# A projection step between the second and third query tile of each FoX score block, and the GLA query/key projection cut into two-bank pieces

## The chip, the cores and the metric

The kernel runs on one core of one Trainium2 chip. The metric is device microseconds (us) of one execution. The median of three runs of the kernel before is 1455.17 us (1454.29 to 1455.19).

## What is computed

One decoder layer on 512 tokens of width 1024, in float32: a half-step SwiGLU feed-forward network, a token mixer, and a second half-step feed-forward network, each between RMSNorms that are shifted, scaled and gated by a conditioning vector. The token mixer has two branches that read the same normed input `h`. Cut to what matters here:

```python
z = h @ w_in      # columns: GLA q,k,v,low-rank gate,out-gate | FoX q,k,v,forget | merge gates
logf = log_sigmoid(f_b + b_f);  F = cumsum(logf)
# FoX, 16 heads of 64, in query blocks of 128:
s = einsum('bhqd,bhkd->bhqk', q, k) * hd ** -0.5 + F[..., None] - F[:, :, None, :]
s = where(kpos <= qpos, s, -inf);  o_b = einsum('bhqk,bhkd->bhqd', softmax(s), v)
# GLA, 4 heads of 128: chunked gated linear attention o_a from q_a, k_a, v_a
merged = sigmoid(gate_a) * (o_a @ w_pa) + sigmoid(gate_b) * (o_b @ w_pb)
y = merged @ w_out
```

## The kernel before

Every large product is made of three float32r products (high by high, high by low, low by high part), each a 128x128 weight against 512 columns. Weights arrive by DMA on the SyncE queue into `raw` (four buffers), ScalarE rounds them to `whi` (L155), VectorE subtracts to `wlo` (L156), TensorE multiplies (helper `mm3`, L192; L378 in the feed-forward part).

**PSUM.** Eight banks: six rotate under the name `mm` (`acc`), two under `aux`. A new `mm` tile takes the next bank of the six, and its first matmul waits until the last reader of that bank is done.

**The filler list.** All projections of the token mixer that don't depend on the attention are cut into steps of 12 matmuls of 512 columns and put in one list, the class `Fill`. `F.run(n)` emits the next n steps and `F.until(mark)` emits steps up to a mark; the code calls these between the pieces of the attention. `F.tr` (L577) makes a projection of two tiles in 4 steps and holds two `mm` banks over them; with four tiles (as in `F.qk`, L594) it takes 8 steps and holds four banks. `F.extra` adds a step that sums one quarter of the modulation vectors: on TensorE it is 8 tiny matmuls (L268). In the list the FoX query/key projections of head pairs 1 to 7 follow each other in 4 steps each, and in front of pairs 1, 3, 5 and 7 stands one extra step.

**One head pair of FoX.** There are eight head pairs; "(k)" below means pair k. Four pieces of code work on it.

- *parts(k)* (L613, run by `evacuate`): reads the two projected banks and makes the high and low halves of q and k for both heads, on ScalarE (L617, L619, L623) and VectorE (L618, L620, L622), head 0 and then head 1.
- *scores(k)* (`fox_scores`, L728): for each of four query tiles and both heads two matmuls (L749, L750) of 128, 256, 384 and 512 columns into one `mm` bank, so eight banks in a row out of six. VectorE adds the decay bias and takes the row maximum (L753), which frees the bank.
- *soft(k)* (`fox_soft`): exponentials on ScalarE (L762), normalisation on VectorE (L766).
- *turn(k)* (`fox_turn`, L778: 18 transposes, copied by ScalarE, L780) and *out(k)* (`fox_out`, L789: the product with v; ScalarE rounds it, L198, VectorE subtracts, L199).

The main loop over p (L846 on) runs soft(p), one step, scores(p+1), steps up to a mark, turn(p), one step, out(p), parts(p+2), one more step. So two steps of the list stand between parts(p+2) and scores(p+2). The engines run their queues in order. The framework's scheduler has ordered each queue from this program order, and the order of the built program can differ from that of the code by some matmuls; every queue shown below is that of the built program.

Of the kernel before, what the change touches and what calls it, by code (L numbers as in the profile page):

```python
# [12 lines left out]
AF = mybir.ActivationFunctionType  # L13
ALU = mybir.AluOpType

P = 128
# [3 lines left out]
KD = D // P  # L20
# [3 lines left out]
QA, KA, VA, AL, RA, QB, KB, VB, FB, GA, GB = (  # L24
    0, 512, 1024, 2048, 2064, 3088, 4112, 5136, 6160, 6176, 7200)
# [14 lines left out]
def tile_hybrid_layer(  # L40
# [4 lines left out]
    nc = tc.nc  # L45
    x, out = x[0], out[0]
    w_ada, b_ada, g_pre, g_post = w_ada[0], b_ada[0], g_pre[0], g_post[0]
    w_in, w_a2, b_a, b_f, g_gla = w_in[0], w_a2[0], b_a[0], b_f[0], g_gla[0]
# [9 lines left out]
    def nm(s):  # L58
        uid[0] += 1
        return f"{s}_{uid[0]}"  # L60

    def unit(dt=F32, shape=(P, 512)):
        return sb.tile(list(shape), dt, tag="u", bufs=NU, name=nm("u"))

    def tmp(shape=(P, 512), dt=F32):
        return sb.tile(list(shape), dt, tag="t2", bufs=NTMP, name=nm("t2"))
# [4 lines left out]
    def acc(shape=(P, 512)):  # L71
        return pm.tile(list(shape), F32, tag="mm", name=nm("mm"))
# [4 lines left out]
    def small(n, tag="sm", bufs=16):  # L77
        return sb.tile([P, n], F32, tag=tag, bufs=bufs, name=nm(tag))
# [237 lines left out]
    def h_tiles():  # L316
        return [(unit(F32R), unit(F32R)) for _ in range(KD)]
# [119 lines left out]
    hs = h_tiles()  # L437
# [86 lines left out]
    hs = nxt[-1]  # L524
# [7 lines left out]
    class Fill:  # L532
# [61 lines left out]
        def qk(self, qc, kc, scale, dst):  # L594
# [7 lines left out]
                    dst.append((q, k))  # L602
            self.tr([(w_, e, lambda: hs) for e in range(2) for w_ in (qw, kw)], evac)

        def qk_parts(self, qc, kc, scale, dst):


            qw, kw = Block(w_in, 0, KD, qc, P), Block(w_in, 0, KD, kc, P)

            def evac(ps):  # L610
                late.append(lambda: parts(*ps))

            def parts(q, k):  # L613
                qx, ky, kx = [(unit(F32R), unit(F32R)) for _ in range(3)]
                for e in range(2):
                    n, o = halves[e], halves[1 - e]
                    nc.scalar.copy(ky[e][n], k[n])  # L617
                    nc.vector.tensor_tensor(kx[e][n], k[n], ky[e][n].bitcast(F32), ALU.subtract)  # L618
                    nc.scalar.activation(qx[e][n], q[n], AF.Copy, scale=scale)  # L619
                    nc.vector.scalar_tensor_tensor(qx[e][o], q[n], scale, qx[e][n].bitcast(F32),  # L620
                                                   ALU.mult, ALU.subtract)
                    nc.vector.tensor_copy(kx[e][o], ky[e][n])  # L622
                    nc.scalar.copy(ky[e][o], kx[e][n])  # L623
                dst.append((qx, ky, kx))
            self.tr([(w_, 0, lambda: hs) for w_ in (qw, kw)], evac)

    F = Fill()
# [6 lines left out]
    fqk = []  # L634
# [81 lines left out]
    def packed():  # L716

        return unit(), unit(), unit(F32, (P, 256))

    def s_at(u, i):  # L720

        return (u[1][:, 384:512], u[2], u[1][:, 0:384], u[0])[i]
# [2 lines left out]

        return (u[0], u[1][:, 0:384], u[2], u[1][:, 384:512])[j]

    def fox_scores(p, qx, ky, kx):  # L728
        S, nmx, rs = [], [], []
        for e in range(2):  # L730
            h = 2 * p + e
            fb = tmp()
            nc.sync.dma_start(fb, Fd[h].partition_broadcast(P))
            s = packed()
            for i in range(NT):
                n = (i + 1) * P
                nc.gpsimd.tensor_scalar(s_at(s, i), fb[:, 0:n], -1.0, Ft[:, i, h:h + 1], ALU.mult, ALU.add)  # L737
                dg = s_at(s, i)[:, n - P:n]
                nc.gpsimd.tensor_tensor(dg, dg, mneg, ALU.add)
            S.append(s)  # L740
            nmx.append(small(4))
            rs.append(small(4))
        for i in range(NT):
            n = (i + 1) * P
            sps = []
            for e in range(2):
                ts = slice(i * P, (i + 1) * P)
                sp = acc()
                nc.tensor.matmul(sp[:, 0:n], qx[e][:, ts], ky[e][:, 0:n], start=True, stop=False)  # L749
                nc.tensor.matmul(sp[:, 0:n], qx[e][:, ts], kx[e][:, 0:n], start=False, stop=True)  # L750
                sps.append(sp)
            for e in range(2):
                nc.vector.tensor_tensor_reduce(s_at(S[e], i), sps[e][:, 0:n], s_at(S[e], i), 1.0, -3e38,  # L753
                                               ALU.add, ALU.max, nmx[e][:, i:i + 1])
        return S, nmx, rs

    def fox_soft(state):
        S, nmx, rs = state
        for e in range(2):
            nc.vector.tensor_scalar(nmx[e], nmx[e], -1.0, None, ALU.mult)  # L760
            for i in range(NT):
                nc.scalar.activation(s_at(S[e], i), s_at(S[e], i), AF.Exp, bias=nmx[e][:, i:i + 1],  # L762
                                     accum_out=rs[e][:, i:i + 1])
            nc.vector.reciprocal(rs[e], rs[e])
            for i in range(NT):
                nc.vector.tensor_scalar(s_at(S[e], i), s_at(S[e], i), rs[e][:, i:i + 1], None, ALU.mult)  # L766

    def fox_turn(state):
        S = state[0]
        PT = []  # L770
        for e in range(2):
            pt = packed()
            for js in ((0,), (1, 3), (2,)):
                tp = (acc if e and 0 in js else aux)()
                off = 0
                for j in js:
                    for i in range(j, NT):
                        nc.tensor.transpose(tp[:, off:off + P], s_at(S[e], i)[:, j * P:(j + 1) * P], ident)  # L778
                        off += P
                nc.scalar.copy(pt[(0, 1, 2)[js[0]]][:, 0:off], tp[:, 0:off])  # L780
            PT.append(pt)
        return PT

    def fox_out(p, PT):
        po = acc()
        for j in range(NT):
            for e in range(2):
                h = 2 * p + e
                nc.tensor.matmul(po[64 * e:64 * e + 64, j * P:T], vb[j][h // 8][:, (h % 8) * 64:(h % 8 + 1) * 64],  # L789
                                 p_at(PT[e], j), start=j == 0, stop=j == NT - 1)  # L790
        o = (unit(F32R), unit(F32R))
        hilo(o[0], o[1], po)
        ob.append(o)
# [6 lines left out]
    marks = [F.mark()]  # L800
# [7 lines left out]
    def gate_b(db):  # L808
        gw = Block(w_in, 0, KD, GB + db * 256, 256)

        def evac(ps):
            for p_ in ps:
                g = unit()
                nc.scalar.activation(g, p_, AF.Tanh, scale=0.5)
                gb.append(g)
        F.tr([(gw, 0, lambda: hs), (gw, 1, lambda: hs)], evac)

    def merge_b(db):
        pw = Block(w_pb, 0, KD, db * 256, 256)

        def evac(ps):
            for p_ in ps:
                m = gb[len(mb)]
                nc.vector.scalar_tensor_tensor(m, m, 1.0, p_, ALU.add, ALU.mult)
                mb.append(m)
        F.tr([(pw, 0, lambda: ob), (pw, 1, lambda: ob)], evac)

    gqk = []
    F.qk(QA, KA, P ** -0.5, gqk)
    start_b = F.mark()  # L830
    for db in range(4):
        gate_b(db)
        merge_b(db)
    end_b = F.mark()

    def evacuate():
        while late:
            late.pop(0)()

    F.until(marks[0])  # L840
    evacuate()
    F.until(marks[1])
    st = [fox_scores(0, *fqk[0])]
    evacuate()
    F.run(1)
    for p in range(8):  # L846
        fox_soft(st[p])
        if p < 7:
            F.run(1)
            st.append(fox_scores(p + 1, *fqk[p + 1]))  # L850
        if p < 6:
            F.until(marks[p + 2] - 1)
        elif p == 7:
            F.run(4)
        PT = fox_turn(st[p])
        F.run(1)
        fox_out(p, PT)
        evacuate()
        if p == 5:
            ra2 = tmp()  # L860
            tc.keep_in_program_order(nc.sync.dma_start(ra2[0:16], w_a2))
            wa2, fill_wa2 = stacked((0, 1, 0))
            fill_wa2(ra2[0:16])
        if p < 7:
            F.run(1)

    F.until(start_b + 8)


    B, rest = [], []  # L870
# [179 lines left out]
    for h in range(4):  # L1050
# [4 lines left out]
        def fill(li):  # L1055
            F.run(2 if h == 0 or li < 4 else 1)
            if li == 0 and prev:
                prev.turn()
            if li == 4 and h < 3:
                if h == 1:  # L1060
                    F.until(gqk_end)
                nxt_hd.append(heads[h + 1]())
                nxt_hd[0].prep()
# [77 lines left out]
```

## Time and profile before

| | |
|---|---|
| median of three runs | 1455.17 us |
| the profiled execution | 1452.96 us |
| its span, first to last instruction | 1451.2 us |
| TensorE busy | 1399.9 us, 96% |
| VectorE, ScalarE, GpSimd busy | 765.7, 531.4, 203.8 us |
| mean granted TensorE clock | 0.989 of 2.4 GHz |

All stretches below are us from the start of the span. The feed-forward networks fill 0 to 420 and 1065 to the end. The FoX scores run from 500 to 650. The profile gives a start and a length for every instruction, and for idle time of an engine the event that ended it.

### The profile page before, as it was taken

How to read it: one execution, taken by the hardware profiler on the slowest of the kernel's cores; microseconds unless marked ns; L12 is line 12 of the kernel's file. 1: busy time of each engine (PE TensorE's matmuls, PEld its weight loads, DVE VectorE, ACT ScalarE, POOL GpSimd, SP SyncE). 2: the span in 40 equal slices, each digit the busy share in tenths (PEclk: the TensorE clock that was granted, in tenths of full speed). 3: DMA queues.
4: the chain of work that ended last, by engine and by line, in shares of the span. 5: the costliest groups of instructions: out<-in, count | busy, mean ns of one | idle time of the engine just before them, and what ended most of it. 6: DMA issues, size and time to landing. Idle time of an engine off the chain costs nothing.

```text
span 1451.2 us, 17081 instructions
## 1 busy us (share of the span) xinstructions
PE 1399.9 (96%) x6477; PEld 1124.3 (77%) x6477; DVE 765.7 (53%) x1210; ACT 531.4 (37%) x915; POOL 203.8 (14%) x328
## 2 busy tenths in 40 slices
PE   4899999999999999999999999999999999999998
PEld 3688888878877777767888887788888888887886
DVE  6945544372266689762745546538464334337232
ACT  5332322232244376653723333423353322222221
POOL 6200000000041643340110202100060000000001
PEclk7999999999999999999999999999999999999999
DMA  9444543272235846212232232125613223325411
GB/s 323 156 147 145 156 148 102 59 246 99 90 120 163 241 135 182 82 40 91 87 106 84 59 87 59 59 73 163 204 55 116 87 91 100 100 87 184 136 58 58
DMA packets 156463, 173.36 MB, mean 119 GB/s; under 512 B 8778, under 2 KB 123574, under 8 KB 156380
## 3 DMA queue, kind: packets, MB, share of 16 engines
q1 hardware_dynamic: 156380, 172.26, 38.4%
q8 instruction: 51, 0.84, 0.2%
q14 instruction: 32, 0.26, 0.1%
HBM read 168.00 MB, written 4.23 MB: 119 GB/s over the span
## 4 chain that ended last, share of the span: by engine, by line
PE 56%; DVE 4%; ACT 2%; issue 1%; POOL 1%; DMA 0%; DVEq 0%; POOLq 0%; ACTq 0%
PE mm L192 34%; PE mm L378 16%; PE aux L964 1%; PE aux L778 1%; PE mm L789 1%; DVE wlo L156 1%; ACT u L762 1%; PE mm L749 0%; PE mm L750 0%; DVE t L213 0%; DVE u L766 0%; POOL sm L310 0%; DVE u L753 0%; DMA raw<-in_w_dn_dram 0%; ACT jk L314 0%
## 5 line engine op out<-in xcount | busy, mean ns | idle before, releaser
L156 DVE TENSOR_TENSOR wlo<-raw,whi 128x1024 fp32r<-128x1024 f32 x218 | 271.9, 1250 | 405.1 <-ACT whi L155 397.1
L378 PE MATMUL mm<-u,whi 128*128 128x512 f32 (+1 forms) x1472 | 451.5, 390 | 10.3 <-ACT u L198 9.9
L155 ACT CAST whi<-raw 128x1024 fp32r<-128x1024 f32 x220 | 230.0, 1049 | 540.1 <-PE mm L192 294.8
L192 PE MATMUL mm<-whi,u 128*128 128x512 f32 x1216 | 390.1, 397 | 1.5 <-ACT u L198 1.5
L378 PEld LDWEIGHTS mm<-u,whi 128*128 128x128 f32 x1472 | 274.7, 190 | 75.5 <-ACT u L198 13.0
L192 PE MATMUL mm<-u,whi 128*128 128x512 f32 x896 | 288.2, 401 | 0.8 <-DVE u L991 0.8
L378 PE MATMUL mm<-u,wlo 128*128 128x512 f32 (+1 forms) x736 | 283.3, 389 | 0.0
L192 PEld LDWEIGHTS mm<-whi,u 128*128 128x128 f32 x1216 | 228.2, 188 | 54.2 <-ACT u L198 1.7
L192 PE MATMUL mm<-wlo,u 128*128 128x512 f32 x608 | 240.3, 395 | 0.0
L192 PEld LDWEIGHTS mm<-u,whi 128*128 128x128 f32 x896 | 166.2, 188 | 39.1 <-DVE u L991 1.2
L192 PE MATMUL mm<-u,wlo 128*128 128x512 f32 x448 | 177.9, 397 | 0.0
L378 PEld LDWEIGHTS mm<-u,wlo 128*128 128x128 f32 x736 | 139.5, 190 | 31.0
L192 PEld LDWEIGHTS mm<-wlo,u 128*128 128x128 f32 x608 | 114.2, 188 | 28.0
L192 PEld LDWEIGHTS mm<-u,wlo 128*128 128x128 f32 x448 | 84.4, 188 | 19.7
L307 POOL TENSOR_SCALAR sm<-ss 128x1 f32<-128x1 f32 x12 | 2.3, 190 | 667.1 <-ACT jk L314 667.1
L198 ACT CAST u<-t 128x512 fp32r<-128x512 f32 (+1 forms) x84 | 44.5, 537 | 113.9 <-DVE t L401 78.4
L213 DVE SCALAR_TENSOR_TENSOR t<-raw,csil,t 128x512 f32<-128x512 f32 x98 | 74.6, 762 | 2.7 <-DMA raw<-in_w_ada_dram 0.6
L737 POOL TENSOR_SCALAR u<-t,Ft 128x128 f32<-128x128 f32 (+1 forms) x64 | 41.7, 661 | 95.5 <-DMA t<-Fd 89.2
L400 DVE SCALAR_TENSOR_TENSOR t<-t,mm 128x512 f32<-128x512 f32 x44 | 30.1, 683 | 47.0 <-ACT t L399 47.0
L399 ACT ACTIVATE t<-mm 128x512 f32<-128x512 f32 x44 | 26.1, 594 | 63.3 <-PE mm L378 63.2
L401 DVE SCALAR_TENSOR_TENSOR t<-t,mm 128x512 f32<-128x512 f32 x44 | 30.2, 686 | 31.1 <-PE mm L378 29.4
L199 DVE TENSOR_TENSOR u<-t,u 128x512 fp32r<-128x512 f32 x52 | 35.6, 689 | 16.1 <-ACT u L198 15.9
(176 smaller groups left out, 1123.4 us busy)
## 6 DMA issues: line engine op xcount, KB each, us to landing
raw<-in_w_gu_dram SPq DMA_DIRECT2D x88, 512.0 KB, 3.6
raw<-in_w_in_dram SPq DMA_DIRECT2D x64, 512.0 KB, 3.8
raw<-in_w_dn_dram SPq DMA_DIRECT2D x44, 512.0 KB, 3.5
raw<-in_w_ada_dram SPq DMA_DIRECT2D x64, 256.0 KB, 3.1
raw<-in_w_ada_dram SPq DMA_DIRECT2D x24, 512.0 KB, 3.8
u<-in_w_ada_dram SPq DMA_DIRECT2D x32, 256.0 KB, 6.6
raw<-in_w_in_dram SPq DMA_DIRECT2D x16, 256.0 KB, 3.9
t<-Fd SPq DMA_DIRECT2D x16, 256.0 KB, 4.7
```

The source lines that it names most:

```text
L155: nc.scalar.copy(hi, raw)
L156: (eng or nc.vector).tensor_tensor(lo, raw, hi.bitcast(F32), ALU.subtract)
L192: nc.tensor.matmul(ps, a[i], b[j], start=first and n == 0, stop=last and n == 2)
L198: nc.scalar.copy(hi, src)
L199: (eng or nc.vector).tensor_tensor(lo, src, hi.bitcast(F32), ALU.subtract)
L213: nc.vector.scalar_tensor_tensor(a, raw[:, j, :], csil[:, k:k + 1], a, ALU.mult, ALU.add)
L378: nc.tensor.matmul(p_[:, ts], w_[k][i][:, cs], hs[k][e][:, ts], start=ks[0] == 0 and n == 0, stop=ks[-1] == KD - 1 and n == 3 * len(ks) - 1)
L399: nc.scalar.activation(th, pg, AF.Tanh, scale=0.5)
L400: nc.vector.scalar_tensor_tensor(th, th, 1.0, pg, ALU.add, ALU.mult)
L401: nc.vector.scalar_tensor_tensor(th, th, 0.5, pu, ALU.mult, ALU.mult)
L737: nc.gpsimd.tensor_scalar(s_at(s, i), fb[:, 0:n], -1.0, Ft[:, i, h:h + 1], ALU.mult, ALU.add)
L762: nc.scalar.activation(s_at(S[e], i), s_at(S[e], i), AF.Exp, bias=nmx[e][:, i:i + 1], accum_out=rs[e][:, i:i + 1])
```

## The change

It makes three edits.

- `fox_scores` takes a function `fill` and calls it once before the third query tile (i == 2). Every caller passes one step of the filler list. The step that stood after `evacuate`, at the end of each pass of the main loop, is gone in return, and so is the step before the first scores. One step, and no longer two, stands between parts(p+2) and scores(p+2), and another within scores(p+2).
- The first half of the GLA query/key projection, one call of `F.qk` with four banks and 8 steps, becomes two calls of the new `qk_one` with two banks and 4 steps each.
- The merge gate `gate_b(0)` moves in the list ahead of it; the marks are counted anew, so that the whole list has the same length and the work after the loop starts with the same step as before.

```diff
+        def qk_one(self, qc, kc, scale, dst):
+            qw, kw = Block(w_in, 0, KD, qc, P), Block(w_in, 0, KD, kc, P)
+
+            def evac(ps):
+                q, k = unit(), unit()
+                nc.scalar.activation(q, ps[0], AF.Copy, scale=scale)
+                nc.scalar.copy(k, ps[1])
+                dst.append((q, k))
+            self.tr([(w_, 0, lambda: hs) for w_ in (qw, kw)], evac)
...
-    def fox_scores(p, qx, ky, kx):
+    def fox_scores(p, qx, ky, kx, fill):
...
         for i in range(NT):
+            if i == 2:
+                fill()
             n = (i + 1) * P
...
-    F.qk(QA, KA, P ** -0.5, gqk)
+    gate_b(0)
+    for e in range(2):
+        F.qk_one(QA + e * P, KA + e * P, P ** -0.5, gqk)
     start_b = F.mark()
     for db in range(4):
-        gate_b(db)
+        if db:
+            gate_b(db)
         merge_b(db)
...
-    F.until(marks[1])
-    st = [fox_scores(0, *fqk[0])]
+    F.until(marks[1] - 1)
+    st = [fox_scores(0, *fqk[0], lambda: F.run(1))]
     evacuate()
     F.run(1)
     for p in range(8):
         fox_soft(st[p])
         if p < 7:
             F.run(1)
-            st.append(fox_scores(p + 1, *fqk[p + 1]))
+            st.append(fox_scores(p + 1, *fqk[p + 1], lambda: F.run(1)))
         if p < 6:
             F.until(marks[p + 2] - 1)
-        elif p == 7:
-            F.run(4)
+        else:
+            F.run(1 if p == 6 else 4)
         PT = fox_turn(st[p])
...
-        if p < 7:
-            F.run(1)
-
-    F.until(start_b + 8)
+
+    F.until(start_b + 4)
```

In the changed kernel the lines move: L749 and L750 become L762 and L763, L753 becomes L766, L762 becomes L775, L778 becomes L791, L789 becomes L802, L617 to L623 become L627 to L633.

**TensorE between out(0) and scores(2), before.** `mm_3877` is the bank of out(0), `mm_3944` a bank of the projection of pair 3, `mm_3988` the first bank of scores(2); `u_3890` and `u_3892` are head 0's q and k from parts(2).

```order
L789 MATMUL mm_3877<-u_3826,u_3074 64x128
L789 MATMUL mm_3877<-u_3845,u_3074 64x128
L268 MATMUL aux_3910<-ones,t_696_3672 128x1 x4
L192 MATMUL mm_3944<-u_2850,whi_3729 128x512
L192 MATMUL mm_3944<-u_2851,whi_3729 128x512
...
L192 MATMUL mm_3944<-u_2861,whi_3729 128x512
L749 MATMUL mm_3988<-u_3892,u_3890 128x128
```

**The same place in the changed kernel.** `aux_4055` is the first piece of turn(1), `mm_3968` and `mm_3971` are the first banks of scores(2) for heads 0 and 1, `mm_3990` is the projection of pair 3.

```order
L802 MATMUL mm_3877<-u_3826,u_3074 64x128
L802 MATMUL mm_3877<-u_3845,u_3074 64x128
L268 MATMUL aux_3930<-ones,t_696_3672 128x1 x4
L791 MATMUL aux_4055<-ident,u_3748 128x128
...
L791 MATMUL aux_4055<-ident,u_3747 128x128
L762 MATMUL mm_3968<-u_3892,u_3890 128x128
L763 MATMUL mm_3968<-u_3894,u_3890 128x128
L762 MATMUL mm_3971<-u_3893,u_3891 128x128
...
L763 MATMUL mm_3979<-u_3895,u_3891 128x256
L192 MATMUL mm_3990<-u_2850,whi_3729 128x512
```

Before, 17 projection matmuls stand between L268 and the first score matmul, and 7 more between head 0 and head 1. Now four transposes stand there and no projection matmul; the 12 of `mm_3990` follow the first two query tiles. Scores(4) and scores(6) have the same form, with seven transposes. At scores(3), (5) and (7) the built program has 13 projection matmuls ahead of head 0 and 6 or 7 ahead of head 1, where before 24 stood ahead of them.

**ScalarE at the same place of the changed kernel,** from the rounding of out(0) to the last piece of parts(2).

```order
L775 ACTIVATE u_3762,sm_3774<-u_3762,sm_3773 128x512
L198 CAST u_3886<-mm_3877 128x512
L155 CAST whi_4238<-raw_4236 128x1024
L627 CAST u_3892<-mm_3694 64x512
L629 ACTIVATE u_3890<-mm_3693 64x512
L633 COPY u_3892<-u_3894 64x512
L627 CAST u_3893<-mm_3694 64x512
L629 ACTIVATE u_3891<-mm_3693 64x512
L633 COPY u_3893<-u_3895 64x512
```

This sequence is the one of before: exponentials of soft(1), the rounding of out(0), one weight block, then parts(2). At scores(4) and (6) of the changed kernel it has the same form, the weight block included; before, no weight block stood between the rounding and parts(4) or parts(6).

## Rows read from the trace of the kernel before

**Rows 1.** Page: busy engines; the last chain by engine; a DMA group

```profile
PE 1399.9 (96%) x6477; PEld 1124.3 (77%) x6477; DVE 765.7 (53%) x1210; ACT 531.4 (37%) x915; POOL 203.8 (14%) x328
...
PE 56%; DVE 4%; ACT 2%; issue 1%; POOL 1%; DMA 0%; DVEq 0%; POOLq 0%; ACTq 0%
...
raw<-in_w_in_dram SPq DMA_DIRECT2D x16, 256.0 KB, 3.9
```

**Rows 2.** Windows: us, PE, PEld, DVE, ACT, POOL busy (count), clock, DMA share, GB/s

```profile
500.00:525.00 25.00, 22.20 (x113) 16.83 (x114) 21.43 (x62) 17.26 (x44) 12.25 (x24) 1.00 0.37 115
625.00:650.00 25.00, 21.50 (x98) 16.58 (x97) 17.32 (x45) 12.68 (x32) 10.45 (x18) 0.86 0.07 22
...
700.00:725.00 25.00, 25.00 (x108) 20.12 (x107) 19.26 (x30) 18.07 (x22) 6.34 (x5) 1.00 0.34 103
```

**Rows 3.** Timeline, TensorE, scores(0) and (1): start, length, [idle before <- what ended it]

```profile
503.79 0.44 PE L749 MATMUL mm<-u,u 128*128 128x384 f32 x1 [1.33 <-DVE sm L753]
...
504.94 0.40 PE L750 MATMUL mm<-u,u 128*128 128x512 f32 x1
...
511.75 0.30 PE L749 MATMUL mm<-u,u 128*128 128x128 f32 x1 [0.62 <-DVE u L620]
...
513.96 0.45 PE L749 MATMUL mm<-u,u 128*128 128x384 f32 x1 [0.46 <-DVE sm L753]
```

**Rows 4.** Timeline, TensorE, turn(0) to the sums after out(0)

```profile
518.06 1.03 PE L778 MATMUL aux<-ident,u 128*128 128x128 f32 x8
...
523.72 2.37 PE L789 MATMUL mm<-u,u 128*64 128x512 f32 x16
526.03 1.05 PE L268 MATMUL aux<-ones,t 128*128 128x1 f32 x8
```

**Rows 5.** Timeline, ScalarE, from the end of soft(1) into parts(2)

```profile
525.45 0.71 ACT L762 ACTIVATE u<-u,sm 128x512 f32<-128x512 f32 x1
...
526.16 0.57 ACT L198 CAST u<-mm 128x512 fp32r<-128x512 f32 x1
527.16 1.05 ACT L155 CAST whi<-raw 128x1024 fp32r<-128x1024 f32 x1 [0.43 <-DMA raw<-in_w_in_dram]
528.11 0.58 ACT L617 CAST u<-mm 64x512 fp32r<-64x512 f32 x1
...
530.52 0.58 ACT L617 CAST u<-mm 64x512 fp32r<-64x512 f32 x1
```

**Rows 6.** Timeline, VectorE, parts(2)

```profile
528.11 0.68 DVE L199 TENSOR_TENSOR u<-mm,u 128x512 fp32r<-128x512 f32 x1
...
532.11 0.69 DVE L620 SCALAR_TENSOR_TENSOR u<-mm,u 64x512 fp32r<-64x512 f32 x1
532.72 0.66 DVE L622 CAST u<-u 64x512 fp32r<-64x512 f32 x1
```

**Rows 7.** Timeline: TensorE at scores(3) and out(2); VectorE in parts(4)

```profile
552.87 0.30 PE L749 MATMUL mm<-u,u 128*128 128x128 f32 x1 [0.27 <-DVE u L620]
...
563.83 2.37 PE L789 MATMUL mm<-u,u 128*64 128x512 f32 x16
...
570.49 0.69 DVE L620 SCALAR_TENSOR_TENSOR u<-mm,u 64x512 fp32r<-64x512 f32 x1
```

**Rows 8.** Timeline: TensorE from out(5) to scores(7); VectorE's subtraction after out(5)

```profile
622.09 2.37 PE L789 MATMUL mm<-u,u 128*64 128x512 f32 x16
...
630.90 0.30 PE L749 MATMUL mm<-u,u 128*128 128x128 f32 x1 [0.62 <-DVE u L620]
...
633.13 0.33 PE L749 MATMUL mm<-u,u 128*128 128x128 f32 x1 [1.66 <-ACT u L623]
...
635.53 0.69 PE L749 MATMUL mm<-u,u 128*128 128x384 f32 x1 [1.17 <-DVE sm L753]
...
638.25 0.63 PE L750 MATMUL mm<-u,u 128*128 128x512 f32 x1
...
628.77 0.68 DVE L199 TENSOR_TENSOR u<-mm,u 128x512 fp32r<-128x512 f32 x1
```

## The prediction

> **What bounds the kernel now.** I read the page first: TensorE is busy 96% of the span, and the last chain runs on it for 56%, on VectorE for 4%, on ScalarE for 2%, on DMA for 0% [rows 1]. So the end moves by what TensorE waits and by its clock, nothing else. The windows say where it waits in the part that the change touches: of 25 us it lacks 2.80 in 500 to 525 and 3.50 in 625 to 650, where the granted clock also drops to 0.86 [rows 2]. The timeline names these waits. At scores(0) and scores(1) the third query tile waits 1.33 and 0.46 us for a bank that L753 has to read, and scores(1) waits 0.62 for parts(1) [rows 3]. At scores(7) two waits, 0.62 and 1.66, are for parts(7), and one, 1.17, is for a bank [rows 8]. At scores(3) there is 0.27 for parts(3) [rows 7], and one like it at scores(5). Scores(2), (4) and (6) wait for nothing on TensorE. Two resources thus share these waits: the banks, which the added step relieves, and the halves of q and k, from in front of which a step is taken.
>
> **The bank waits: a gain.** The new step is 12 matmuls; a matmul takes 25/108 = 0.231 us [rows 2], so it covers 2.8 us. The longest bank wait is 1.33, so all three go: 1.33 + 0.46 at the start, 1.17 at scores(7). At scores(1) ScalarE now has two more exponentials (at most the 0.71 of the row of L762 each [rows 5]) ahead of the last piece of parts(1), which otherwise could start earlier; I take the 0.62 to grow by half of 2 x 0.71 less a little, to some 1.2. Net of the start: -1.2 us (from -1.8 to -0.3).
>
> **The step taken away: a loss at scores(2), (4) and (6).** The list has an extra step in front of pairs 3, 5 and 7, and this is the one step now left between parts and scores there: 8 tiny matmuls. Behind out(0) the TensorE queue then holds L268, four transposes, and the first matmul of scores(2), which needs parts(2); what could fill the gap is queued behind it. I follow the two sides from the end of out(0), 523.72 + 2.37 = 526.09 [rows 4].
>
> TensorE: L268 ends at 527.08, +0.99. A transpose is 1.03/8 = 0.13 [rows 4], so four or seven of them end at +1.5 to +1.9; I take +1.7.
>
> Parts(2): ScalarE does the last exponential, then rounds out(0) at 526.16, splits a weight block at 527.16, and only then comes to L617, at 528.11; the one of head 1 follows at 530.52 [rows 5]. VectorE ends q of head 1 (L620) at 532.80, +6.7, and the low half that the second matmul needs (L622) at 533.38, +7.3 [rows 6]. Before, 24 matmuls (5.6 us) covered this. The changed ScalarE queue has the same sequence at all three places, weight block included, so scores(2) is the nearest row; 0.43 of it was a wait for a weight DMA [rows 5], so I take head 1's parts at +6.4. The lower bound is scores(4), where no weight block stood in between: out(2) ended at 566.20 and L620 of head 1 at 571.18, +4.98 [rows 7].
>
> In between TensorE can do only head 0's two matmuls, about 0.35. Idle per place: 6.4 - 1.7 - 0.35 = 4.35; from 4.98 - 1.9 - 0.35 = 2.7 to 7.3 - 1.5 - 0.35 = 5.4. Three places: **+13.0 us (8.2 to 16.3)**. Nothing gives this back: TensorE had no idle there before, and its work is the same.
>
> **The clock: a second loss.** At scores(7) TensorE idled 0.62 + 1.66 + 1.17 = 3.45 within the 5.3 us up to 635.53, and the clock went to 1.2 GHz: the window's 0.86 is (1 - 0.86) x 25 / 0.5 = 7.0 us at half speed [rows 2]. The last two query tiles took 635.53 to 638.88, 3.35 us [rows 8], against 503.79 to 505.34, 1.55, at 2.4 GHz [rows 3]. With the 0.9 us or so of the low stretch that were idle anyway, it cost (7.0 - 0.9)/2 = 3.0. At the three places TensorE would idle 4.35 of some 4.8 us, denser than that, so I expect a fall at each, at (7.0 - 1.3)/2 = 2.85, since a little more of it is idle: **+8.5 us (0 to 10)**. A wait of 1.33 alone brought no fall: the clock of 500 to 525 is 1.00 [rows 2].
>
> The Trainium skill, TensorE: Matmul & The Clock Gate, section "A second HAM failure mode: psum-queue depth-cycling", says that TensorE idling briefly between groups while a kernel cycles through PSUM banks is enough to make the clock go back and forth. That speaks against the form of all seven score blocks, and by it the falls would not stop at three; the trace does not bear it out, since eight-bank score blocks with waits up to 1.33 kept 1.00. It is a rival below.
>
> **Scores(3), (5) and (7).** Here 13 matmuls stand ahead of head 0 and 6 or 7 ahead of head 1: TensorE is at head 0 at 13 x 0.231 = +3.0 and at head 1 at +3.0 + 0.35 + 1.5 = +4.9, against parts of head 1 at +4.98 in the fast case [rows 7]. That leaves the 0.27 or so of before, at scores(3) and (5): +0.1 (-0.5 to +2.5). At scores(7) parts came late, because VectorE reached L199 at 628.77, 4.3 after out(5) ended at 624.46 [rows 8], held up by seven mask casts that alternate with GpSimd. The changed queue has these casts inside scores(6), so they are over by then, and parts(7) should take the fast form: idle 1.0 for 3.45, and no fall, which was 3.0. **-5.4 us (-6.4 to +0.5)**; the upper end is a parts(7) as late as before.
>
> **Edits at nothing.** The two-bank projection has the same matmuls, splits and bytes that are used. Written as 128-column blocks it also fetches four times 256 KB that nobody reads; one takes 3.9 us to land [rows 1], on queues that are used 7% at 625 to 650 [rows 2]. If that cover were gone it would be 4 x 3.9 = 16 us at most, but no TensorE wait in this trace is ended by a weight DMA. The gate evaluated earlier is two activations that ScalarE does while TensorE multiplies.
>
> **The sum.** -1.2 + 13.0 + 8.5 + 0.1 - 5.4 = +15.0 us on the profiled execution's 1452.96. That execution is 2.2 under the median of the three, so against the median I forecast 1455.2 + 15.0 = **1470.2 us**.
>
> **The rivals.**
> - *Waits at the three places, but no fall there.* For it: 1.33 us brought none. Against it: 3.45 of 5.3 did. 1470.2 - 8.5 = 1461.7.
> - *Faster, as the code reads.* Place: ScalarE behind out(0), out(2), out(4). If parts(k) were not held behind the rounding and the weight block, for they need only banks that are complete before out(k-2), they would be ready when TensorE arrives, and the loss is gone: 1455.2 - 1.2 - 5.4 = 1448.6. It decides once the idle per place is under 6.5/3 = 2.2 us. Against it: the built queue, and 2.7 as the quickest row.
> - *Fast parts and no fall:* 1455.2 - 1.2 + 8.2 + 0.1 - 5.4 = 1456.9, no change that can be told.
> - *Scores(7) stays as it was,* wait and fall: 1470.2 + 5.9 = 1476.1.
> - *Falls at scores(3), (5) and (7) as well:* 3 x 2.85 = 8.5 more, 1478.7. The rule of the skill above would give this.
>
> **How the numbers follow.** Forecast 0.45; no fall 0.20; scores(7) as before 0.12; more falls 0.05; faster 0.10; no change 0.08. About 0.2%, 2.9 us, is what a measurement of this kernel can tell from no change. Slower is 0.45 + 0.20 + 0.12 + 0.05 = 0.82, faster 0.10, same 0.08. The range leaves out the faster rival and what lies beyond the most falls: 1456 to 1479.
>
> **What would show it.** Right: on TensorE, idle of 2 us or more ahead of the first score matmul (L762) of scores(2), (4) and (6) and again ahead of head 1, ended by parts (L630, L633); a granted clock under 1.00 in three windows of 525 to 630; no idle ahead of the 384-column tiles; less idle at scores(7). Wrong: a total idle of the three places under 6 us; a clock of 1.00 there; or new waits that weights or `aux` banks end, which the sum doesn't have.

## The result

The changed kernel takes 1468.6 us, median of four runs (1466.5 to 1469.6), beside 1454.7 for the kernel before on the same chip. The ratio is 1.0093 (95% interval 1.008 to 1.0107): 13.9 us slower. The forecast was 1470.2. The profiled execution of after took 1466.5 us, with a span of 1464.8, so its rows show 13.6 us more than those of before.

### The profile page after: what moved, and what is told of

Read it like the earlier page. It is cut to its first block, busy times and chain, and to the rows that moved or that the text cites. A ratio compares the mean times of both kernels' runs of the same rounds, so it can differ in the third digit from the quotient of the medians.

```text
span 1464.8 us, 17085 instructions
## 1 busy us (share of the span) xinstructions
PE 1403.9 (96%) x6477; PEld 1128.2 (77%) x6477; DVE 762.6 (52%) x1210; ACT 532.0 (36%) x915; POOL 203.8 (14%) x328
## 4 chain that ended last, share of the span: by engine, by line
PE 85%; DVE 8%; DMA 3%; issue 2%; ACT 1%; POOL 1%; SPq 0%; DVEq 0%; POOLq 0%; ACTq 0%
PE mm L192 46%; PE mm L378 32%; PE aux L978 1%; DVE wlo L156 1%; DMA u<-in_w_ada_dram 1%; DVE t L213 1%; PE mm L802 1%; PE aux L791 1%; DMA raw<-in_w_dn_dram 1%; PE mm L762 1%; PE mm L763 1%; DVE t L243 1%; ACT jk L314 1%; PE aux L268 1%; POOL sm L310 1%
## 5 line engine op out<-in xcount | busy, mean ns | idle before, releaser
L156 DVE TENSOR_TENSOR wlo<-raw,whi 128x1024 fp32r<-128x1024 f32 x218 | 271.7, 1249 | 403.5 <-ACT whi L155 394.4
L155 ACT CAST whi<-raw 128x1024 fp32r<-128x1024 f32 x220 | 230.3, 1049 | 563.1 <-PE mm L192 321.1
L192 PE MATMUL mm<-u,whi 128*128 128x512 f32 x896 | 291.8, 405 | 0.8 <-DVE u L1005 0.8
L198 ACT CAST u<-t 128x512 fp32r<-128x512 f32 (+1 forms) x84 | 44.5, 537 | 113.8 <-DVE t L401 78.2
L775 ACT ACTIVATE u<-u,sm 128x128 f32<-128x128 f32 (+1 forms) x64 | 35.1, 553 | 26.0 <-DVE sm L773 26.0
```

The lines of the kernel that those rows point to most:

```text
L155: nc.scalar.copy(hi, raw)
L156: (eng or nc.vector).tensor_tensor(lo, raw, hi.bitcast(F32), ALU.subtract)
L192: nc.tensor.matmul(ps, a[i], b[j], start=first and n == 0, stop=last and n == 2)
L198: nc.scalar.copy(hi, src)
```

## The profile after

The first group answers [rows 1]: busy engines, the last chain by engine, and the 256 KB weight fetches, now 20 for 16.

```profile
PE 1403.9 (96%) x6477; PEld 1128.2 (77%) x6477; DVE 762.6 (52%) x1210; ACT 532.0 (36%) x915; POOL 203.8 (14%) x328
...
PE 85%; DVE 8%; DMA 3%; issue 2%; ACT 1%; POOL 1%; SPq 0%; DVEq 0%; POOLq 0%; ACTq 0%
...
raw<-in_w_in_dram SPq DMA_DIRECT2D x20, 256.0 KB, 3.1
```

TensorE is still 96% busy and ends the program. The twenty fetches land in 3.1 us each (median; 3.9 before). What the four unread ones cost is measured below, in the run with the list alone.

To see where the 13.6 us lie, cut a stretch between two fixed matmuls: the first of the low-rank gate projection (L649, in the changed kernel L659) and the first that uses `wa2` (L873, now L887). In all kernels below the same matmuls lie between them, save in one that adds some. This is the windows view of that stretch in before (columns as in [rows 2]: bounds, length, then PE, PEld, DVE, ACT and POOL busy, clock, DMA share, GB/s):

```profile
448.92:689.00 240.08, 231.91 (x1142) 179.22 (x1141) 162.49 (x376) 129.63 (x281) 80.37 (x150) 0.99 0.46 135
```

The same stretch in after:

```profile
448.26:701.96 253.70, 235.57 (x1141) 182.86 (x1140) 159.00 (x376) 129.99 (x281) 80.19 (x150) 0.95 0.45 132
```

The stretch grew from 240.08 to 253.70, all of the 13.6. TensorE's idle time in it went from 240.08 - 231.91 = 8.17 to 253.70 - 235.57 = 18.13, +10.0; its busy time, for the same matmuls, by +3.7, with the clock down from 0.99 to 0.95.

The waits of TensorE in after from 480 to 680 (line that waited, releaser, us in total, times, longest); before had those of [rows 3, 7, 8] there:

```profile
PE mm L762 <- DVE u L630: 16.5, 7, 3.5
```

All waits for a bank (L753, now L766) and for the last piece of parts (L623, now L633) are gone. L762's waits for L630, the last piece of q, are 16.5 us in seven waits. The timeline of TensorE at scores(2) and scores(4) shows four of them (start, length, [idle before <- releaser]):

```profile
523.18 1.05 PE L268 MATMUL aux<-ones,t 128*128 128x1 f32 x8
524.10 0.63 PE L791 MATMUL aux<-ident,u 128*128 128x128 f32 x4
528.22 0.45 PE L762 MATMUL mm<-u,u 128*128 128x128 f32 x1 [3.48 <-DVE u L630]
...
530.52 0.77 PE L762 MATMUL mm<-u,u 128*128 128x128 f32 x2 [1.58 <-DVE u L630]
...
532.01 1.05 PE L192 MATMUL mm<-u,whi 128*128 128x512 f32 x2
...
570.34 1.18 PE L791 MATMUL aux<-ident,u 128*128 128x128 f32 x8
574.19 0.30 PE L762 MATMUL mm<-u,u 128*128 128x128 f32 x1 [2.67 <-DVE u L630]
...
577.23 0.77 PE L762 MATMUL mm<-u,u 128*128 128x128 f32 x2 [2.47 <-DVE u L630]
```

Behind the sums (L268) and the transposes (L791) TensorE idles 3.48, does head 0's two matmuls, and idles 1.58 again: 5.06 us. At scores(4) it is 2.67 + 2.47 = 5.14, at scores(6) 2.67 + 2.32 = 4.99: 15.2 us in all. The seventh wait is at scores(1), 1.32 us for 0.62 [rows 3]. Scores(3), (5) and (7) have no wait over 0.2.

The windows answer [rows 2]:

```profile
500.00:525.00 25.00, 23.39 (x127) 18.14 (x125) 23.24 (x67) 19.11 (x48) 11.90 (x24) 1.00 0.47 135
525.00:550.00 25.00, 20.20 (x96) 15.89 (x96) 16.67 (x46) 13.46 (x31) 12.74 (x22) 0.86 0.61 171
550.00:575.00 25.00, 21.88 (x122) 16.55 (x118) 21.20 (x53) 16.04 (x37) 6.88 (x12) 1.00 0.56 165
575.00:600.00 25.00, 22.77 (x104) 17.80 (x104) 14.02 (x38) 12.54 (x32) 12.45 (x24) 0.86 0.28 78
600.00:625.00 25.00, 19.75 (x111) 15.22 (x110) 15.38 (x46) 15.13 (x36) 4.79 (x12) 0.89 0.30 90
625.00:650.00 25.00, 24.99 (x113) 19.01 (x113) 16.79 (x43) 12.58 (x30) 16.32 (x35) 0.90 0.27 81
```

Between 500 and 650 the clock of 1.00 is lost at scores(2), (4) and (6) alone. At scores(2) matmuls from 528 to 534 run at 1.2 GHz: the two `whi` matmuls that follow the 256-column tiles take 1.05 us, where such a pair takes 0.63 at 2.4 GHz.

## Experiments

Each is an edit of the changed kernel unless it says otherwise. "The stretch" is the one cut above, out of the run's own profile.

### Put back the step that was taken away

```diff
+        if p < 6:
+            F.run(1)
```

(at the end of each pass of the main loop)

> The changed kernel with the one step put back that it takes from the end of each pass of the main loop: only the added step within the scores and the new two-bank pieces are left. My theory (what loses is the cover taken from in front of scores(2), (4) and (6)): 24 matmuls again stand between out(p) and the second head of the next scores, so the 15.2 us of idle that TensorE has at these three places in the changed kernel fall to under 0.5 each, the clock stays at 1.00 from 525 to 630, no bank wait returns and scores(7) keeps its gain: 1448 to 1451. Rival (the step within the scores or the two-bank pieces cost the time themselves, by contention or by what they trigger): no more than a third of the loss goes, about 1464.

Measured: 1452.6 us, ratio 0.9986 (0.9977 to 0.9996).

The stretch in the windows of this run:

```profile
452.28:689.90 237.62, 229.06 (x1141) 176.70 (x1140) 161.09 (x376) 129.84 (x281) 82.85 (x150) 1.00 0.48 141
```

And the waits of TensorE from 510 to 660:

```profile
PE mm L762 <- DVE u L630: 4.9, 6, 1.9
PE mm L762 <- ACT u L633: 1.2, 2, 0.7
PE mm L762 <- DVE sm L766: 0.7, 1, 0.7
```

All of the loss is gone, and no matmul of the stretch ran below 1.00. What is left is a little over the 0.5 us per place expected: 0.18 ahead of head 0 and 0.27 + 0.41 at head 1 of scores(2), 0.68 at head 1 of scores(4) and 0.67 at head 1 of scores(6). The one at scores(4) is for a bank (L766), and no bank wait was expected. So the step within the scores makes no loss by itself. But it gains 2 us, not the 4 to 7 expected: 1.91 and 0.51 us of wait for parts(7) are back at scores(7), and 1.61 us at scores(1).

### Two projection steps ahead of scores(2), (4) and (6)

```diff
-            F.run(1)
+            F.run((2, 3)[p % 2])
```

(ahead of scores(p+1): two steps more ahead of scores(2), (4) and (6), and one more ahead of each other block from scores(1) on, which the expectation leaves out)

> The changed kernel with one step more run ahead of scores(2), (4) and (6) alone, and the list that much earlier at its end. If cover ahead of the scores is all that lacks, it must not matter from where the step is taken: idle at the three places under 0.5 each, no falls of the clock, 1447 to 1451. Rival (it is the total number of steps that are in place around the turn and the product with v that matters, not the two between parts and scores): idle of 2 us or more per place stays, 1460 or more.

Measured: 1451.7 us, ratio 0.998 (0.9969 to 0.999). No wait over 0.25 us is left at scores(2) to (6); the wait at scores(7) is 2.85, with a short fall of the clock behind it. In the built program 36 projection matmuls stand ahead of these three blocks and 24 ahead of scores(3), (5) and (7), where the kernel before has 20 to 24 ahead of head 1 of each. So cover ahead of the scores is enough, wherever it is taken from; that the same amount would do at this place as at the end of the pass isn't shown, since this run has more. The time is just over the upper end expected, and again scores(7) is what keeps it there.

### The removal alone

```diff
-            if i == 2:
-                fill()
...
-    F.until(marks[1] - 1)
+    F.until(marks[1])
```

> The changed kernel without the step within the scores: the step taken away at the end of each pass, alone. My theory: the idle at scores(2), (4) and (6) and the clock falls there are as in the changed kernel (15 us and three falls), and the bank waits at scores(0), (1) and (7) come back on top (2 to 3 us): 1469 to 1473. Rival (the fill itself makes the wait, since its 12 matmuls keep parts or banks back): the idle at the three places falls to under 2 us each, 1455 to 1460.

Measured: 1467.4 us, ratio 1.0087 (1.007 to 1.0104). The removal alone makes the whole loss. The split within it is not the expected one: idle at scores(2) is 4.92, but 1.93 and 1.92 at scores(4) and (6), and yet the clock fell at all three, and once more at scores(7). The stretch is 253.37 long, as after, with 238.82 busy and 14.55 idle: less idle time than after (18.13), and more busy time at the low clock. That the two totals agree is thus in part chance. Why parts(4) came earlier is to be read in the timeline of ScalarE, here of this run:

```profile
571.03 1.07 ACT L155 CAST whi<-raw 128x1024 fp32r<-128x1024 f32 x1
573.09 0.59 ACT L198 CAST u<-mm 128x512 fp32r<-128x512 f32 x1 [0.99 <-PE mm L800]
```

and here of the changed kernel:

```profile
569.62 0.57 ACT L198 CAST u<-mm 128x512 fp32r<-128x512 f32 x1
570.09 1.05 ACT L155 CAST whi<-raw 128x1024 fp32r<-128x1024 f32 x1
571.04 0.58 ACT L627 CAST u<-mm 64x512 fp32r<-64x512 f32 x1
```

In this run the scheduler put the weight block (L155) ahead of the rounding (L198), in time in which ScalarE waited for out(2) anyway. In the changed kernel it stands between the rounding and L627.

### Parts ahead of the product with v

```diff
+        evacuate()
         fox_out(p, PT)
-        evacuate()
```

> The changed kernel with the code of parts(p+2) moved ahead of out(p), nothing else. My theory says that parts(2), (4), (6) come late because they are queued behind the rounding of out(p) and a weight block on ScalarE; put ahead of them they are interleaved with the last exponentials of the pair before and are ready when TensorE arrives: idle per place 0 to 1.5 us for 5, no fall, 1448 to 1455. Rival (parts are late by their own length or by VectorE, whatever stands ahead of them): idle of 4 us or more per place stays, 1466 to 1470; or the exponentials, now later, make turn and out wait instead, the same time at another line.

Measured: 1461.5 us, ratio 1.0042 (1.003 to 1.0054), between the theory and its rival. Idle at the three places fell from 15.2 to 2.04 + 2.47 + 2.89 = 7.4; head 0 of the scores no longer waits at any of them. What is left are these waits, from 520 to 660:

```profile
PE mm L762 <- DVE u L630: 3.4, 3, 2.5
PE aux L791 <- DVE u L779: 1.5, 2, 1.3
PE aux L791 <- DVE scc L277: 1.5, 1, 1.5
PE mm L762 <- ACT u L793: 1.4, 1, 1.4
PE mm L762 <- ACT u L633: 1.3, 1, 1.3
```

So about half of the wait was parts' place behind out(p). Of what is left, 2.47 us at scores(4) and 0.49 at scores(2) are still waits for head 1's parts, in which ScalarE and VectorE take turns. The rest is new: transposes that wait for the normalisation (L779) or for an `aux` bank (L277), and scores behind a transpose's copy (L793). Parts had been moved ahead of these. The clock still fell at all three places, and also at scores(7), behind 0.44 and 1.31 us (the L633 of the list) of wait for parts(7).

### A projection step for the tiny one

```diff
         F.qk_parts(QB + p * P, KB + p * P, 0.125, fqk)
+        if p % 2:
+            F.steps.insert(len(F.steps) - 3, F.steps.pop(-5))
```

> The changed kernel with the same number of steps at every call, but the tiny step (the modulation sums, L268 of before) of pairs 3, 5 and 7 set behind the first two steps of its pair in the list and no longer in front of them. The one step left between parts and scores is then always 12 matmuls of 512 columns. My theory: the loss is there because the one step left at scores(2), (4) and (6) is the tiny one; with a projection step in its place TensorE arrives as late as at scores(3) and (5) of the changed kernel, where nothing over 0.2 us is lost: idle per place under 1 us, no falls of the clock, 1450 to 1455. Rival (one step instead of two is the loss, whatever it holds): 12 matmuls are 2.8 us of the 7.1 that parts take after out, so 2 us or more of idle per place stay, and 1458 to 1464.

Measured: 1456.4 us, ratio 1.0009 (0.9998 to 1.002). At the three places it went as the theory says: waits of 0.72, 0.67 and 0.67, clock 1.00, with one step between parts and scores as in the changed kernel. The time is 1.4 us over its range, by waits elsewhere: 2.17 at scores(1) and 2.55 at scores(7), both with a fall of the clock, and 1.3 to 2.0 at scores(3) and (5). So what counts is what the one step holds. How much 12 matmuls alone would cover isn't told apart: in the built program nine more, of the step within the scores, stand ahead of head 0 as well, and eight transposes ahead of head 1.

### The clock's share

```diff
+            if p in (1, 3, 5):
+                w = aux()
+                for n_ in range(14):
+                    nc.tensor.matmul(w, ob[-1][0][:, 0:P], hs[n_ % KD][0], start=True, stop=True)
```

(and eight more between head 0 and head 1 of the first query tile)

> The changed kernel with extra matmuls whose result nobody reads, in TensorE's queue where it waits: 14 of 512 columns ahead of scores(2), (4) and (6), and 8 between head 0 and head 1 of their first query tile. They fill the waits (5.1 us per place) without ending them sooner, so the time differs from the changed kernel's by the clock alone. My theory: the clock stays at 1.00, the score blocks start at the same time as in the changed kernel, and the low stretches' cost is saved: by the trace of after 3.4 to 8 us for the three, so 1460 to 1465. Rival (the low clock costs nothing that counts, since work behind it is not bound by TensorE): 1467 to 1470.

Measured: 1464.4 us, ratio 1.0063 (1.0049 to 1.0076); 4.2 us under the changed kernel. At scores(4) and (6) head 0 and head 1 start 4.7 and 7.7 us after the end of out(p) in both kernels: the wait is the same, only filled. At scores(2) head 1 starts at +7.6, for +7.3 in after. What follows differs. These are the windows from head 1's first matmul to the first 384-column tile, the same matmuls each time, at scores(2), (4) and (6) of after:

```profile
530.52:535.85 5.33, 5.33 (x19) 4.53 (x19) 4.64 (x14) 0.39 (x1) 4.46 (x7) 0.64 0.69 185
577.23:583.01 5.78, 5.78 (x18) 4.83 (x19) 1.59 (x9) 0.88 (x2) 4.30 (x9) 0.58 0.58 173
624.00:630.23 6.23, 6.23 (x19) 5.19 (x19) 2.36 (x12) 0.88 (x2) 2.02 (x9) 0.53 0.50 153
```

And in this run:

```profile
531.64:535.84 4.20, 3.80 (x19) 3.12 (x19) 4.17 (x14) 0.00 (x0) 3.43 (x7) 1.00 0.61 162
577.83:581.48 3.65, 3.65 (x19) 3.10 (x20) 1.51 (x9) 0.00 (x0) 2.20 (x4) 1.00 0.89 268
623.19:626.80 3.61, 3.61 (x19) 3.07 (x19) 1.98 (x11) 0.00 (x0) 1.04 (x5) 1.00 0.58 182
```

TensorE is busy 17.34 us in the first three and 11.06 in the others, so the low clock costs 6.3 us (1.5, 2.1 and 2.6). The rival, a low clock that costs nothing, fails. The time fell by less, 4.2 us, and the stretch by 3.65 (250.05 for 253.70). An estimate of the rest: 14 transposes of 0.13 us [rows 4] that after does within its waits come behind them in this run, 1.8 us, and at scores(2) head 1 starts 0.3 later and waits 0.40 once more.

### The list alone

```diff
-            if i == 2:
-                fill()
...
+        if p < 7:
+            F.run(1)
```

(and the calls of the loop as before)

> The loop of before with the new list alone: the two-bank pieces of the GLA projection and the gate ahead of them. My theory: nothing at scores(2) to (6) changes, since their steps are the old ones; at scores(7) the waits for parts(7) depend on where the mask casts fall, so 1452 to 1456. Rival (the two-bank pieces, with their unread weights, are part of the changed kernel's loss): over 1458.

Measured: 1454.5 us, ratio 1.0003 (0.9994 to 1.0012). The two-bank pieces, their unread fetches and the earlier gate are worth nothing either way. The waits at scores(7) are those of [rows 8]: 0.65, 1.65 and 1.17.

### The mask casts

Four kernels move the code that builds the seven masks of the GLA part. It alternates between GpSimd and VectorE, and the scheduler had drawn it into the last score blocks. First the kernel before with this code, which stood behind the main loop, ahead of the scores:

```diff
+    masks = sb.tile([P, len(LEVELS), 256], U8, tag="masks", name="masks")
+    for li, Lv in enumerate(LEVELS):
...
     F.until(marks[0])
```

> The kernel before with one edit: the seven masks that GpSimd builds and VectorE casts for the GLA part are made ahead of the FoX scores in the code, where the built program puts them long before scores(0). My reading of before: the two waits for parts(7) (0.62 and 1.66 us) and the fall of the clock at scores(7) come from VectorE standing in these casts. Then without them: waits of scores(7) for parts under 1 us in all, no fall there, 1449 to 1452. Rival (parts(7) are late for another reason, or the casts cost as much at their new place): 1453.5 or more, with the waits of scores(7) as before.

Measured: 1451.6 us, ratio 0.998 (0.997 to 0.999). At scores(7) no wait for parts is left and the clock is 1.00. At their new place the casts made the first transposes of the mixer wait 2.39 us (1.1 in before, and in e10 and e11 below), and the clock fell there. Then the same with the step in the scores and two steps of cover:

> The added step within the scores, two projection steps of cover ahead of scores(2), (4) and (6) as in the run e2, and the masks built early. If the 2.85 us wait that e2 keeps at scores(7) is the casts', it goes, and with it the fall of the clock: idle between 495 and 660 under 2.5 us, no low clock between 100 and 1400, 1446 to 1449. If the wait at scores(7) stays for another reason: 1450 to 1452, like e2.

Measured: 1451.7 us, ratio 0.9975 (0.9965 to 0.9986): no gain over e2. The expectation failed, though not as its other branch says: scores(7) had no wait any more, but there were 2.39 us at the first transposes (1.1 in e2) and a fall of the clock there, and one more fall at 315 us, in the feed-forward network. The stretch is still shorter than that of e2 in the profiled executions (236.09 for 237.98), so why the medians agree stays open. So both were built with the masks in the first feed-forward network:

> The run e8 with the masks built still earlier, in the first feed-forward network, where TensorE has no idle and VectorE is half free. In e8 they cost 2.39 us at the first transposes of the mixer and a fall of the clock there. If that is their price at that place, it goes: 1446 to 1449. If the gain does not add up because something else then ends last: 1450 to 1452, like e8.

> The kernel before with the masks built in the first feed-forward network, and nothing of the change. If the change's two real gains (bank waits and scores(7)) come from the masks' place for the most part, this is as fast as e10 within 1 us: 1448 to 1451. If the added step and its cover give their own 2 to 3 us of bank waits, e10 is faster by that much.

```diff
-    extra = [lambda ch=ch: mod_cols(sh2, sc2, 1, ch) for ch in range(4)]
+    extra = [lambda ch=ch: ch == 1 and build_masks() or mod_cols(sh2, sc2, 1, ch) for ch in range(4)]
```

Measured: e10 1448.2 us, ratio 0.9954 (0.994 to 0.9967); e11 1448.8 us, ratio 0.9962 (0.9949 to 0.9974). Both beat the kernel before and the changed one. The mask casts as a group of their line (count, shortest/median/longest ns, first and last start), in before:

```profile
L894 DVE CAST masks<-t x7: 282/293/584, 615.2 to 625.1; 128x256 uint8<-128x256 f32 x7
```

In after:

```profile
L908 DVE CAST masks<-t x7: 285/293/583, 626.1 to 637.9; 128x256 uint8<-128x256 f32 x7
```

In e11 they run from 110.7 to 115.5.

The windows view of the stretch in e11:

```profile
448.70:682.42 233.72, 228.38 (x1141) 176.57 (x1140) 158.78 (x369) 129.69 (x281) 73.52 (x129) 1.00 0.47 139
```

and in e10:

```profile
451.00:684.57 233.57, 230.32 (x1141) 179.17 (x1140) 158.40 (x369) 131.15 (x281) 73.67 (x129) 1.00 0.49 144
```

Against before, e11 moves nothing but the casts: idle in the stretch falls from 8.17 to 5.34, and busy time from 231.91 to 228.38. Not all of the latter is the fall of the clock at scores(7): among kernels without any fall in the stretch the busy time goes from 228.38 to 230.32. The fall alone is read at the same 42 matmuls from the first 384-column tile of scores(7) on, in before:

```profile
635.53:645.62 10.09, 10.09 (x42) 8.48 (x44) 3.69 (x17) 5.23 (x15) 0.00 (x0) 0.70 0.01 2
```

and in e11:

```profile
631.34:639.05 7.71, 7.63 (x42) 5.93 (x44) 3.36 (x17) 5.16 (x15) 0.00 (x0) 1.00 0.01 2
```

So that fall cost 2.4 us. The stretch is no shorter in e10, and its lead over e11 (0.6 us) is within the intervals: once the casts are away, the added step has nothing left to gain that these runs can tell.

## Why the prediction was right, and where its terms were not

**Right:** the sign, the places and the mechanism. The loss comes from the step taken away ahead of scores(2), (4) and (6) (removal alone: 1467.4; step put back: 1452.6), TensorE waits there for parts, and the clock falls at these three places and nowhere else between 500 and 660. The sum was 15.0, the measurement 13.9. That it came so close is luck in part: the idle time was 2.2 us more than forecast and the clock's cost 2.2 us less, and the two cancelled.

- **Start,** forecast -1.2: the bank waits of 1.33 and 0.46 went and scores(1) grew from 0.62 to 1.32, -1.1.
- **Idle at the three places,** forecast 13.0: 15.2. TensorE arrived as reckoned, +1.5 us after out(0) and +2.0 after out(2) and out(4), where eight transposes stand ahead and not seven; parts were later. I took head 1's parts at +6.4 us after out(p); scores' head 1 started at +7.3, +7.7 and +7.7. The step that failed is how +6.4 was made from the row of before. It takes off the 0.43 us that ScalarE waited for a weight DMA; at scores(2) of after this wait is 1.23, as the timeline of ScalarE shows:

```profile
525.11 1.04 ACT L155 CAST whi<-raw 128x1024 fp32r<-128x1024 f32 x1 [1.23 <-DMA raw<-in_w_in_dram]
```

So a weight fetch stands in the path to scores(2), which the sum had at nothing. The same wait is 1.26 and 1.32 us in e1 and e5, which have the step within the scores, and 0.44 in e4, which hasn't; why it grows isn't shown. At scores(4) and (6) no weight is waited for, and VectorE holds parts back, as its timeline in parts(4) of after shows:

```profile
571.33 0.69 DVE L199 TENSOR_TENSOR u<-mm,u 128x512 fp32r<-128x512 f32 x1
571.93 0.81 DVE L779 TENSOR_SCALAR u<-u,sm 128x384 f32<-128x384 f32 x2
572.65 0.68 DVE L628 TENSOR_TENSOR u<-mm,u 64x512 fp32r<-64x512 f32 x1
...
574.41 1.23 DVE L156 TENSOR_TENSOR wlo<-raw,whi 128x1024 fp32r<-128x1024 f32 x1
...
576.39 0.69 DVE L630 SCALAR_TENSOR_TENSOR u<-mm,u 64x512 fp32r<-64x512 f32 x1
```

The last subtraction of head 1 (L630, 576.39) stands behind the subtraction of out(2) (L199), two normalisations (L779), and, between head 0 and head 1, a low half of weights (L156, 1.23 us). The first three had their like in the row of before; the low half of weights is what the row didn't have. The upper bound, +7.3, was the truer row.
- **The clock,** forecast +8.5: 6.3, counted at the same matmuls with and without the fall (e5). The low stretches were no shorter than the 7.0 us I took (7.0, 7.0 and 10.5 from the windows above), but I let only 1.3 us of each be free of cost. Waits within a low stretch cost nothing more, and neither do head 0's two matmuls, which end in a wait: what counts is the low time from head 1 on, by the windows of after under e5 (1 - 0.64) x 5.33 / 0.5 = 3.8, 4.9 and 5.9 us. The rival without falls fails.
- **Scores(3) and (5),** forecast +0.1: the 0.27 and its like went, -0.5.
- **Scores(7),** forecast -5.4: -5.9, the 3.45 of idle [rows 8] and 2.4 of clock (e11), for the 2.45 and 3.0 that I took. The casts were indeed what made parts(7) late, and in the changed kernel they ran from 626 to 638, well ahead of scores(7) at 647. I had kept 1.0 us of idle there; none is left. The gain, though, hangs on where the scheduler puts the casts: in e1, e2 and e7, with the same added step, the last cast starts at 628.7 to 630.6, about where out(5) ends, and waits of 1.9 to 2.9 us for parts(7) came back. For e2 the run e8 shows that the casts make this wait; for e1 and e7 it is inferred.
- **Edits at nothing:** shown by the list alone, 1454.5.

These five terms give -1.1 + 15.2 + 6.3 - 0.5 - 5.9 = 14.0 for the stretch's 13.6. The difference of 0.4 is less than what kernels without any fall differ by in busy time (228.38 to 230.32).

**The rule of the Trainium skill** (TensorE: Matmul & The Clock Gate, "A second HAM failure mode: psum-queue depth-cycling"), by which falls would come at scores(3), (5) and (7) as well: here they didn't, the clock is 1.00 from 550 to 575, with scores(3) in it, and in the windows 595 to 610 (scores(5)) and 640 to 660 (scores(7)), though these blocks go through the banks in the same way. It is no full test, since TensorE hardly idles in these three blocks. No run shows a fall at a score block that has no wait of its own.

**The faster rival** failed, by idle per place of 5.1 us for its 2.2. Its idea, parts that are not held in the queues, was half true: e3 halves the wait.

## To carry over

Before moving filler work away from a wait that the trace doesn't show, count what the filler's steps are: a step of tiny matmuls covers next to nothing (here 1.0 us, where a step of 12 matmuls of 512 columns covers 2.8), and the wait behind it is as long as the producers' queues on all engines, and the weight fetches they wait for, not only the queue that was looked at. Where a step is moved, follow the code that a scheduler may draw into the gap (here mask casts that alternate between two engines); taking that out of the critical stretch was worth more (5.5 us) than the added step with all its cover (2 to 3 us, e1 and e2). Price a fall of the clock only by the matmuls in the low stretch that no wait follows, not by its length.

## What the runs showed of the hardware

Whether TensorE's clock falls is not told by the length of a wait alone. In the run e1 the wait of 1.91 us ahead of scores(7) stood behind 512-column matmuls, and the granted clock stayed at 2.4 GHz. In e4 a wait of 1.57 stood behind out(2), eight one-column sums and four transposes, and the clock went to 1.2 GHz. The window of e1:

```profile
625.00:650.00 25.00, 22.50 (x115) 16.69 (x114) 17.82 (x47) 16.24 (x42) 12.53 (x24) 1.00 0.16 43
```

its timeline of TensorE:

```profile
634.55 0.40 PE L192 MATMUL mm<-u,wlo 128*128 128x512 f32 x1
636.86 0.30 PE L762 MATMUL mm<-u,u 128*128 128x128 f32 x1 [1.91 <-DVE u L630]
```

the window of e4:

```profile
570.00:585.00 15.00, 13.07 (x63) 9.97 (x62) 12.15 (x35) 8.36 (x18) 4.02 (x9) 0.77 0.77 223
```

and its timeline of TensorE:

```profile
570.64 2.38 PE L800 MATMUL mm<-u,u 128*64 128x512 f32 x16
572.94 1.05 PE L268 MATMUL aux<-ones,t 128*128 128x1 f32 x8
573.86 0.64 PE L789 MATMUL aux<-ident,u 128*128 128x128 f32 x4
576.06 0.45 PE L760 MATMUL mm<-u,u 128*128 128x128 f32 x1 [1.57 <-DVE u L630]
```

That it was the short matmuls that made the difference was not tried. In e7 waits of 2.17 and 2.55 behind 512-column matmuls did bring falls.
